# A third set of halves for the expert blocks, a later gelu and a planned transfer rate of 430 for 460 in a PEER decoder block

## The chip, the cores and the metric

The kernel runs on one core of one Trainium2 chip. The metric is device time in microseconds (us), the median of several executions. A profiled execution gives the trace; its span is a little shorter than the time of the same run. Engines are called as in the profile: PE is TensorE's matmul stream and PEld its weight loads, DVE is VectorE, ACT is ScalarE, POOL is GpSimd, SP issues transfers; POOLq, ACTq and SPq are their queues of transfers.

## The reference

One residual layer over 1024 tokens of width 1024, in float32. Three token mixers (stick-breaking attention, dilated window attention, attention into 256 memory tokens) run on a normalised input and are merged by gates. Then comes the expert part, which this change is about:

```python
q = (hf @ w_q).reshape(T, 8, 2, 128)
sc = einsum('thpd,hpkd->thpk', q, subkeys)          # 128 keys a half
s1, i1 = top_k(sc[:, :, 0], 16); s2, i2 = top_k(sc[:, :, 1], 16)
top_s, pos = top_k(all 256 sums s1 + s2, 16)        # 16 experts of 16384 a head
gate = softmax(top_s)
act = gelu(einsum('chkd,cd->chk', u[ic], hc))       # 128 rows of u for every token
out = einsum('chk,chkd->cd', gate * act, v[ic])     # and 128 rows of v
```

So each of the 1024 tokens picks 128 rows (4 KB each) out of the tables u and v, 64 MB each.

## The kernel before

**Two ways through the experts.** The tokens lie in 8 tiles of 128. For six tiles the kernel gathers: a *step* is one chosen expert for each of the 128 tokens, so there are 128 steps a tile and 768 in all. A step fetches a 512 KB block of u rows by an indirect transfer from POOL's queue (`fetch`), multiplies it by the tokens on DVE with a sum (`u<-u,h`, L1129), and 34 steps later (`VLAG`) fetches the v rows; `sum` (L1163) adds four v blocks at a time into two PSUM banks, `poa` and `pob`, on PE with small weights `wz`. Such four are called a group here; there are 192. The gathered rows lie in five u and eight v buffers (`UP`, `VP`), and POOL takes its transfers strictly in the program's order.

For the other two tiles (`DENSE`) the kernel reads both whole tables in 128 blocks of 128 experts: `product` multiplies a block of u with the 256 tokens (24 matmuls, L1184, 128x256), ACT takes the gelu of it (`w<-bank`), `weigh` multiplies it with the gates on DVE, and 12 matmuls 128x512 (L1184 again) add the weighted block of v into four banks. These matmuls are fp32r in three terms, so every operand is split into a high and a low half: ACT copies the high one (`uh`, `vh`, `wh`), DVE subtracts for the low one (`ul`, `vl`, L1264, and `wl`, L1335). The raw blocks `ur` and `vr` come by SP in pairs, 1 MB each, two buffers each; the halves have two buffers each. Blocks 0 to 21 (`RUN`) are multiplied earlier without a split (`early`, fp32 matmuls), so `product(e + 22)` and the v part of block e stand in one round of the loop. In a round ACT has, in this order: `uh` of the next block, the gelu of this one, `wh` and `vh` for the next sum. DVE has `ul`, the gate product `w<-w,g`, `wl` and `vl` for the next sum, and between them the `u<-u,h` of the gather.

**What sets the order.** A planner runs while the program is written. It keeps two clocks, one for PE (`pe`) and one for the transfers (`dma`), and before each step of the gather it puts in dense work until the PE clock has caught up with the other:

```python
least = LEAST * ((len(ex.todo) > 0) + (len(ex.vs) > 0))
due = max(due + least, pe - least)
while filler[0] is not None and (dma > pe or pe < due):
    a, b = fill(1)      # a: PE ns of one piece of dense work, b: its bytes / bw
    pe += a
    dma += b
ex.step()
pe += SUM_NS * (ex.sums - n)
dma += ROW_BYTES * (ex.rows - fetched) / bw[0]
```

`BW = 305.0, 460.0` are the planned rates in bytes a ns: the first until the mixers are done (`front.close()`), the second from there on. ACT and POOL keep the order that the planner writes; PE, DVE and SP are ordered by the framework's scheduler near it. All engines run their own order strictly.

**The gelu of a set.** After every 32 steps a set's 32 activations get their gelu on ACT (`gelu`, `gel<-parts`), are scaled and turned on PE, and become the weights `wz`. In the mixers' time ACT otherwise uses Exp and Ln, so a gelu there stands between two loads of an activation table (L127).

**List buffers.** `sc` (two buffers of 8 KB a partition) holds the key scores of `select`; they are idle once the lists of the last tile are made (`side` is empty).

Of the kernel before, what the change touches and what calls it, by code (L numbers as in the profile page):

```python
# [7 lines left out]
F32 = mybir.dt.float32  # L8
# [9 lines left out]
D = 1024  # L18
# [9 lines left out]
F32R = mybir.dt.float32r  # L28
# [6 lines left out]
RUN = 22  # L35


BW = 305.0, 460.0
SLOW = 1.38, 1.1
SUM_NS, ROW_BYTES = 520.0, 128 * 4096 + 12 * 1024.0  # L40
LEAST = 1500.0
# [38 lines left out]
def block_kernel(ctx: ExitStack, tc: tile.TileContext, io):  # L80
# [4 lines left out]
    sc = pool("sc", 2)  # L85
# [24 lines left out]
    def bank():  # L110
        return ps.tile([128, 512], F32, name="bank")

    def mm(out, lhsT, rhs, **kw):
        n = 1
        for d in rhs.shape[1:]:
            n *= d
        cost[0] += 4 * (n / 2.4 + 2.5) * out.shape[0] / 128
        nc.tensor.matmul(out, lhsT, rhs, **kw)  # L118
# [5 lines left out]
    def actf(out, in_, f, **kw):  # L124
        s = SETS.get(f)
        if s and table[0] != s:
            nc.scalar.preload_act_table_set(s)  # L127
            table[0] = s
        nc.scalar.activation(out, in_, f, **kw)  # L129
# [106 lines left out]
    def load(out, src):  # L236
        count(out)
        nc.sync.dma_start(out, src)
# [836 lines left out]
    class Experts:  # L1075
# [46 lines left out]
        def step(self):  # L1122

            self.run_behind()
            if not self.todo:
                return
            t, k = self.todo.pop(0)
            u = self.us.pop(0)
            nc.vector.scalar_tensor_tensor(u, u, 1.0, t["h"], op0=OP.mult, op1=OP.mult,  # L1129
                                           accum_out=t["parts"][:, k:k + 1])  # L1130
            b, c, j = k // 32, k % 32 // QB, k % QB
            self.behind.append([None] * (VLAG - 1) + [lambda: self.fetch("v", t["iT"][:, c, j, b:b + 1])]
                               + [None] * (SLAG - VLAG - 1) + [(lambda: self.sum(t, b, c, j)) if j % SUMS == SUMS - 1 else None])
            if k % 32 == 31:
                self.behind.append([lambda: self.gelu(t, b), lambda: self.scale(t, b), None,
                                    lambda: self.turn(t), lambda: self.weights(t, 0)])

        def gelu(self, t, b):
# [93 lines left out]
    C = 2  # L1232

    def dense():
        st = ctx.enter_context(ExitStack())
        dp = st.enter_context(tc.tile_pool(name="dp", bufs=2))
        late_pool.append(dp)
        while len(stored) < ND:
            cost[0] += 1500
            yield  # L1240
        wait[0] = True
        whole = dp.tile([128, C, D], F32, name="vr")
        for i in range(ND):
            load(whole[:, i].rearrange("p (k t) -> p k t", k=KD), h2d[i])
        hh = dp.tile([128, KD, TD], F32R, name="hh", bufs=1)
        hl = dp.tile([128, KD, TD], F32R, name="hl", bufs=1)

        def split_tokens():
            for i in range(ND):
                r = whole[:, i].rearrange("p (k t) -> p k t", k=KD)  # L1250
                c = slice(i * 128, (i + 1) * 128)
                actf(hh[:, :, c], r, AF.Copy)
                nc.vector.tensor_sub(hl[:, :, c], r, hh[:, :, c])

        def raw(src, name):
            r = dp.tile([128, C, D], F32, name=name)
            load(r, src)
            return r

        def split(r, x, name):  # L1260
            hi = dp.tile([128, D], F32R, name=name + "h")
            lo = dp.tile([128, D], F32R, name=name + "l")
            actf(hi, r[:, x], AF.Copy)
            nc.vector.tensor_sub(lo, r[:, x], hi)  # L1264
            return hi, lo

        ur, us, ws, vr, gts = {}, {}, {}, {}, {}

        def near(e):
            if e % C == 0:  # L1270
                ur[e // C + 1] = raw(io["uT"][e // C + 1], "ur") if e + C < 128 else None
            return ur[e // C]

        def take(e):
            us[e] = split(near(e), e % C, "u")

        def early(e):
            a = bank()[:, :TD].rearrange("p (i t) -> p i t", i=ND)
            u = near(e)
            for k in range(KD):  # L1280
                mm(a, u[:, e % C, k * 128:(k + 1) * 128], whole[:, :, k * 128:(k + 1) * 128], start=k == 0,
                   stop=k == KD - 1)
            w = ws[e] = dp.tile([128, TD], F32, name="w", bufs=RUN + 2)
            actf(w.rearrange("p (i t) -> p i t", i=ND), a, AF.Gelu)

        def product(e, a):
            if e + 1 < 128:
                take(e + 1)
            uh, ul = us.pop(e)
            for k in range(KD):  # L1290
                kc = slice(k * 128, (k + 1) * 128)
                mmr(a, uh[:, kc], hh[:, k, :], start=k == 0, stop=False, skip_group_check=True)
                mmr(a, ul[:, kc], hh[:, k, :], start=False, stop=False, skip_group_check=True)
                mmr(a, uh[:, kc], hl[:, k, :], start=False, stop=k == KD - 1, skip_group_check=True)
            w = ws[e] = dp.tile([128, TD], F32, name="w", bufs=RUN + 2)
            actf(w, a, AF.Gelu)

        def gate_load(b):
            if b < 16:
                gts[b] = dp.tile([128, TD // 32, 8, 32], F32, name="g")  # L1300
                load(gts[b], gd[:, :, 8 * b:8 * b + 8, :].rearrange("b p i t -> p b i t"))

        ur[0] = raw(io["uT"][0], "ur")
        e = steps = 0
        while next(gates) < ND:
            steps += 1
            cost[0] += 800
            if e < RUN and steps % 5 == 0:
                early(e)
                e += 1  # L1310
            yield
        split_tokens()
        early(e)
        gate_load(0)
        vr[0] = raw(io["vd"][0], "vr")
        for e in range(e + 1, RUN):
            yield
            early(e)
        take(RUN)
        yield  # L1320
        behind[0], wait[0] = True, False

        sums = [[bank() for _ in range(2)] for _ in range(ND)]
        ab = bank().rearrange("p (x n) -> p x n", x=2)

        def weigh(e):
            if e % 8 == 0:
                gate_load(e // 8 + 1)
            w = ws.pop(e)
            nc.vector.tensor_mul(w.rearrange("p (b t) -> p b t", t=32), w.rearrange("p (b t) -> p b t", t=32),  # L1330
                                 gts[e // 8][:, :, e % 8, :])
            wh = dp.tile([128, TD], F32R, name="wh")
            wl = dp.tile([128, TD], F32R, name="wl")
            actf(wh, w, AF.Copy)
            nc.vector.tensor_sub(wl, w, wh)  # L1335
            if e % C == 0:
                vr[e // C + 1] = raw(io["vd"][e // C + 1], "vr") if e + C < 128 else None
            return wh, wl, *split(vr[e // C], e % C, "v")

        now = weigh(0)  # L1340
        for e in range(128):
            if e + RUN < 128:
                product(e + RUN, ab[:, e % 2, :])
                yield
            nxt = weigh(e + 1) if e < 127 else None
            wh, wl, vh, vl = now
            for i in range(ND):
                c = slice(i * 128, (i + 1) * 128)
                for half in range(2):
                    o = sums[i][half]  # L1350
                    f = slice(half * 512, (half + 1) * 512)
                    mmr(o, wh[:, c], vh[:, f], start=e == 0, stop=False, skip_group_check=True)
                    mmr(o, wh[:, c], vl[:, f], start=False, stop=False, skip_group_check=True)
                    mmr(o, wl[:, c], vh[:, f], start=False, stop=e == 127, skip_group_check=True)
                yield
            now = nxt
        for i in range(ND):
            r = dp.tile([128, C, D], F32, name="ur")[:, 0]
            load(r, xres[DENSE[i]])
            for half in range(2):  # L1360
                f = slice(half * 512, (half + 1) * 512)
                nc.vector.tensor_add(r[:, f], r[:, f], sums[i][half])
            nc.sync.dma_start(io["out"][DENSE[i]], r)

    ready, side, stored, late_pool, chosen = [], [], [], [], []
# [11 lines left out]
    def rest():  # L1377
# [15 lines left out]
        front.close()  # L1393
        slow[0], bw[0] = SLOW[1], BW[1]
        yield from dense()

    filler = [rest()]
    slow, bw = [SLOW[0]], [BW[0]]
    pe = dma = due = 0.0
# [14 lines left out]
    while ex.done < NT - ND or filler[0] is not None:  # L1414
        if ex.more():
# [3 lines that stand above are left out]
                a, b = fill(1)  # L1419
                pe += a  # L1420
                dma += b
            n = ex.sums
# [4 lines left out]
        else:  # L1427
            a, b = fill(1)
# [56 lines left out]
```

## Time and profile before

| | |
|---|---|
| time, median of 3 | 3656.19 us (3655.71 to 3662.34) |
| profiled execution: its time, its span | 3664.29 us, 3662.5 us |
| busy in the span: PE, DVE, ACT, POOL | 87%, 63%, 27%, 48% |
| moved | 1182.29 MB, mean 323 GB/s |
| of it by POOL's queue (gathered rows) | 805.40 MB, 221184 packets |
| of it by SP's queue | 336.37 MB |

The profiled execution took 1.8 us more than its span, and 8.1 us more than the median of the runs. Times below are in us from the start of the span. In the views, a stretch's row gives the busy us of each engine with the number of its instructions, the clock that TensorE was granted as a share of full speed, the mean busy share of the 16 DMA engines and the GB/s that they moved. In a row of waits the engine and line that waited stand on the left, and what came last on the right, with the total, the number of times and the longest.

### The profile page before, as it was taken

To read this page: it belongs to the slowest core of one execution; us is meant where nothing else is said; L and a number is where in the kernel's file an instruction comes from. 1 tells how busy PE (TensorE), PEld (TensorE's weight loads), DVE (VectorE), ACT (ScalarE), POOL (GpSimd) and SP (SyncE) were. 2 spreads that over 40 slices of the span, in tenths; PEclk is the share of its full clock that TensorE was granted. 3 is DMA by queue.
4 is the path that set the end of the run, shared out by engine and by line. 5 is a ranking of instruction groups with operands and counts; after the bars stand their busy time and mean duration, and the time that the engine had idled before them with its cause. 6 is when DMAs were issued, how large, how long until landed. Compare 5 with 4: busy or idle time off the path is not lost.

```text
span 3662.5 us, 59007 instructions
## 1 busy us (share of the span) xinstructions
PE 3182.7 (87%) x22418; PEld 2381.9 (65%) x22418; DVE 2295.9 (63%) x5873; ACT 994.8 (27%) x2065; POOL 1764.4 (48%) x1543
## 2 busy tenths in 40 slices
PE   7999979988999889899889898946867888889899
PEld 6889856655556666666555557734655767777677
DVE  5443597555444568886655554889756766666645
ACT  4442223332100123342322111111222333333334
POOL 0000046645565555566454555356656665655540
PEclk9999989998999999999999999968888999999999
DMA  4435678989899997899887999879999999999995
GB/s 160 123 117 169 209 250 327 370 308 342 307 384 366 391 348 278 309 343 374 299 317 279 364 360 377 300 277 393 389 387 398 410 409 402 379 385 392 382 358 180
DMA packets 343084, 1182.29 MB, mean 323 GB/s; under 512 B 38480, under 2 KB 79952, under 8 KB 323344
## 3 DMA queue, kind: packets, MB, share of 16 engines
q0 software_dynamic: 221184, 805.40, 58.2%
q1 hardware_dynamic: 100848, 336.37, 25.2%
q10 hardware_dynamic: 20768, 36.74, 2.6%
q8 instruction: 177, 2.90, 0.3%
q14 instruction: 107, 0.88, 0.1%
HBM read 1140.61 MB, written 37.75 MB: 322 GB/s over the span
## 4 chain that ended last, share of the span: by engine, by line
PE 46%; DMA 17%; DVE 13%; issue 13%; POOL 5%; ACT 2%; another core or an unknown queue 2%; ACTq 0%; SPq 0%; POOLq 0%; DVEq 0%
PE bank L118 31%; PE bank L1184 8%; DMA u<-in_u,iI 7%; DMA v<-in_v,iT 6%; DVE u L1129 3%; POOL v L1085 3%; PE poa L1163 3%; PE pob L1163 3%; POOL u L1085 2%; PE bank L122 1%; DMA ur<-in_uT 1%; DMA w<-in_w_gate 1%; ACT e L129 1%; DVE ab L1208 1%
## 5 line engine op out<-in xcount | busy, mean ns | idle before, releaser
L1085 POOL DMA_INDIRECT u<-in_u,iI x768 | 881.0, 1147 | 950.8 <-DVE wide L330 471.9
L1129 DVE SCALAR_TENSOR_TENSOR u<-u,h 128x1024 f32<-128x1024 f32 x768 | 933.3, 1220 | 605.8 <-DMA u<-in_u,iI 508.9
L1085 POOL DMA_INDIRECT v<-in_v,iT x768 | 882.7, 1149 | 853.1 <-PE pob L1163 349.5
L118 PE MATMUL bank<-wide,w 128*128 128x384 f32 x1536 | 523.3, 495 | 14.2 <-DVE wide L330 5.3
L118 PEld LDWEIGHTS bank<-wide,w 128*128 128x128 f32 x1536 | 292.3, 193 | 219.1 <-issue 21.3
L118 PE MATMUL bank<-w,wide 128*128 128x128 f32 x2304 | 277.2, 279 | 20.4 <-issue 17.5
L118 PEld LDWEIGHTS bank<-w,wide 128*128 128x128 f32 x2304 | 267.7, 194 | 35.4 <-issue 28.0
L1163 PE MATMUL pob<-v,wz 128*32 128x256 f32 x3072 | 231.8, 414 | 66.7 <-DMA v<-in_v,iT 61.0
L1184 PE MATMUL bank<-hh,uh 128*128 128x256 f32 x848 | 244.3, 288 | 30.4 <-ACT uh L129 19.0
L1184 PE MATMUL bank<-vl,wh 128*128 128x512 f32 x512 | 212.5, 415 | 51.4 <-DVE vl L1264 42.1
L118 PE MATMUL bank<-big,w 128*128 128x256 f32 (+1 forms) x1280 | 244.1, 347 | 10.7 <-issue 9.1
L1184 PE MATMUL bank<-hh,ul 128*128 128x256 f32 x848 | 243.0, 287 | 11.6 <-DVE ul L1264 10.6
L1163 PE MATMUL poa<-v,wz 128*32 128x256 f32 x3072 | 217.8, 405 | 29.1 <-DMA v<-in_v,iT 20.9
L1184 PE MATMUL bank<-hl,uh 128*128 128x256 f32 x848 | 242.0, 285 | 0.0
L118 PEld LDWEIGHTS bank<-big,w 128*128 128x128 f32 x1280 | 210.0, 196 | 43.7 <-issue 21.6
L129 ACT ACTIVATE e<-bank 128x512 f32<-128x512 f32 (+2 forms) x208 | 110.0, 529 | 448.2 <-PE bank L118 296.2
L1184 PE MATMUL bank<-vh,wh 128*128 128x512 f32 x512 | 212.2, 415 | 0.7 <-ACT vh L129 0.7
L1184 PE MATMUL bank<-vh,wl 128*128 128x512 f32 x512 | 208.3, 407 | 0.0
L1163 PEld LDWEIGHTS pob<-v,wz 128*32 128x32 f32 x3072 | 101.1, 117 | 162.3 <-issue 61.8
L129 ACT ACTIVATE w<-bank 128x256 f32<-128x256 f32 x128 | 49.1, 385 | 573.9 <-PE bank L1184 412.1
L1184 PEld LDWEIGHTS bank<-hh,uh 128*128 128x128 f32 x848 | 164.8, 194 | 40.5 <-ACT uh L129 19.1
L1163 PEld LDWEIGHTS poa<-v,wz 128*32 128x32 f32 x3072 | 98.4, 115 | 124.4 <-issue 47.6
(292 smaller groups left out, 5508.8 us busy)
## 6 DMA issues: line engine op xcount, KB each, us to landing
ur<-in_uT SPq DMA_DIRECT2D x64, 1024.0 KB
vr<-in_vd SPq DMA_DIRECT2D x64, 1024.0 KB
w<-in_w_in SPq DMA_DIRECT2D x102, 512.0 KB
w<-in_w_gate SPq DMA_DIRECT2D x72, 512.0 KB
w<-in_w_pq SPq DMA_DIRECT2D x48, 512.0 KB
g<-gd SPq DMA_DIRECT2D x16, 1024.0 KB
w<-in_w_o SPq DMA_DIRECT2D x48, 256.0 KB
w<-in_w_out SPq DMA_DIRECT2D x24, 512.0 KB
```

The source lines that it names most:

```text
L118: nc.tensor.matmul(out, lhsT, rhs, **kw)
L122: nc.tensor.transpose(out, in_, ident)
L129: nc.scalar.activation(out, in_, f, **kw)
L1085: nc.gpsimd.indirect_dma_start(out=t, out_offset=None, in_=io[kind], in_offset=bass.IndirectOffsetOnAxis(ap=ap, axis=0))
L1129: nc.vector.scalar_tensor_tensor(u, u, 1.0, t["h"], op0=OP.mult, op1=OP.mult, accum_out=t["parts"][:, k:k + 1])
L1163: nc.tensor.matmul(o[32 * k:32 * k + 32], t["wz", c][:, x, :], vs[y][:, 256 * k:256 * k + 256], start=b == 0 and x == SUMS - 1 and c % 2 == 0,
L1184: nc.tensor.matmul(out, lhsT, rhs, **kw)
L1208: nc.vector.tensor_scalar(ab[:, 0, x], iota, sl[:, 0, t + x:t + x + 1], sl[:, 2, t + x:t + x + 1], op0=OP.is_equal, op1=OP.mult)
```

## The change

It has three parts.

1. The halves of a u block are made two blocks ahead and not one: `product(e)` calls `take(e + 2)`, and `take(RUN + 1)` is added at the start. The halves of v likewise, in a new `take_v`, which `weigh(e)` calls for block e + 1. Blocks whose number leaves 2 when divided by 3 put both halves into one `sc` buffer, once `side` is empty; until then, and for the other blocks, the two buffers of before are used.
2. The planned rate `BW[1]` is 430 and not 460.
3. The gelu of a set, and what follows from it, come two steps later.

```diff
-BW = 305.0, 460.0
+BW = 305.0, 430.0
...
             if k % 32 == 31:
-                self.behind.append([lambda: self.gelu(t, b), lambda: self.scale(t, b), None,
+                self.behind.append([None, None, lambda: self.gelu(t, b), lambda: self.scale(t, b), None,
                                     lambda: self.turn(t), lambda: self.weights(t, 0)])
...
-        def split(r, x, name):
-            hi = dp.tile([128, D], F32R, name=name + "h")
-            lo = dp.tile([128, D], F32R, name=name + "l")
+        def split(r, x, name, n):
+            if n % 3 == 2 and not side:
+                both = sc.tile([128, 16, 128], F32, name="sc").rearrange("p a b -> p (a b)").bitcast(F32R)
+                hi, lo = both[:, :D], both[:, D:]
+            else:
+                hi = dp.tile([128, D], F32R, name=name + "h")
+                lo = dp.tile([128, D], F32R, name=name + "l")
             actf(hi, r[:, x], AF.Copy)
             nc.vector.tensor_sub(lo, r[:, x], hi)
             return hi, lo
...
         def product(e, a):
-            if e + 1 < 128:
-                take(e + 1)
+            if e + 2 < 128:
+                take(e + 2)
...
         take(RUN)
+        take(RUN + 1)
...
+        vs = {}
+
+        def take_v(e):
+            if e % C == 0:
+                vr[e // C + 1] = raw(io["vd"][e // C + 1], "vr") if e + C < 128 else None
+            vs[e] = split(vr[e // C], e % C, "v", e)
...
             actf(wh, w, AF.Copy)
             nc.vector.tensor_sub(wl, w, wh)
-            if e % C == 0:
-                vr[e // C + 1] = raw(io["vd"][e // C + 1], "vr") if e + C < 128 else None
-            return wh, wl, *split(vr[e // C], e % C, "v")
-
+            if e + 1 < 128:
+                take_v(e + 1)
+            return wh, wl, *vs.pop(e)
+
+        take_v(0)
         now = weigh(0)
```

POOL's order is the same in both programs. Over the whole program DVE does the 768 `u<-u,h` in both, and its first `vl` stands behind 582 of them in both. From there the orders part. On DVE, in the middle of the dense part, two rounds read so before (`u,parts<-u,h` is the gather's product, the others belong to the dense blocks; the numbers tell buffers apart):

```order
L1264 TENSOR_TENSOR ul_25620<-ur_25422,uh_25619 128x1024
L1129 SCALAR_TENSOR_TENSOR u_25670,parts_21863<-u_25670,h_21861 128x1024
L1330 TENSOR_TENSOR w_25647<-w_25647,g_26461 128x256
L1335 TENSOR_TENSOR wl_25679<-w_24181,wh_25678 128x256
L1264 TENSOR_TENSOR vl_25683<-vr_25459,vh_25682 128x1024
L1264 TENSOR_TENSOR ul_25706<-ur_25559,uh_25705 128x1024
L1129 SCALAR_TENSOR_TENSOR u_25675,parts_21863<-u_25675,h_21861 128x1024
L1129 SCALAR_TENSOR_TENSOR u_25695,parts_21863<-u_25695,h_21861 128x1024
L1330 TENSOR_TENSOR w_25733<-w_25733,g_26461 128x256
L1335 TENSOR_TENSOR wl_25742<-w_24241,wh_25741 128x256
L1129 SCALAR_TENSOR_TENSOR u_25738,parts_21863<-u_25738,h_21861 128x1024
L1264 TENSOR_TENSOR vl_25748<-vr_25601,vh_25747 128x1024
```

and so after, on DVE at the same place:

```order
L1268 TENSOR_TENSOR ul_25109<-ur_24916,uh_25108 128x1024
L1129 SCALAR_TENSOR_TENSOR u_25190,parts_22402<-u_25190,h_22400 128x1024
L1342 TENSOR_TENSOR w_25136<-w_25136,g_25572 128x256
L1347 TENSOR_TENSOR wl_25150<-w_23708,wh_25149 128x256
L1268 TENSOR_TENSOR vl_25154<-vr_24958,vh_25153 128x1024
L1268 TENSOR_TENSOR sc_25199<-ur_25054,sc_25199 128x1024
L1129 SCALAR_TENSOR_TENSOR u_25195,parts_22402<-u_25195,h_22400 128x1024
L1342 TENSOR_TENSOR w_25226<-w_25226,g_26110 128x256
L1347 TENSOR_TENSOR wl_25230<-w_23765,wh_25229 128x256
L1129 SCALAR_TENSOR_TENSOR u_25284,parts_22402<-u_25284,h_22400 128x1024
L1268 TENSOR_TENSOR vl_25236<-vr_25091,vh_25235 128x1024
```

The same two rounds hold four gather products before and three after, and the second `ul` goes into an `sc` buffer (31 blocks of u and 38 of v do). The halves `ul` and `vl` stand at the same places among the others, but are those of the block after the next.

At the end of DVE's order the rows before are these (`ur<-ur,bank` adds the dense sums to the residual):

```order
L1335 TENSOR_TENSOR wl_28271<-w_27804,wh_28270 128x256
L1264 TENSOR_TENSOR vl_28275<-vr_28209,vh_28274 128x1024
L1362 TENSOR_TENSOR ur_28302<-ur_28302,bank_19977 128x512
L1362 TENSOR_TENSOR ur_28302<-ur_28302,bank_19978 128x512
L1362 TENSOR_TENSOR ur_28307<-ur_28307,bank_19979 128x512
L1362 TENSOR_TENSOR ur_28307<-ur_28307,bank_19980 128x512
L1480 UNCONDITIONAL_BRANCH
```

and after, on DVE at the end (`row<-row` adds a quarter of the gather's last tile, `wz<-wT` makes the weights of its next two groups):

```order
L1176 TENSOR_TENSOR row_27963<-row_27963,poa_24330 128x256
L1153 TENSOR_TENSOR wz_28118<-wT_27904,spread_84 128x256
L1347 TENSOR_TENSOR wl_28034<-w_27320,wh_28033 128x256
L1375 TENSOR_TENSOR ur_28090<-ur_28090,bank_19903 128x512
L1375 TENSOR_TENSOR ur_28090<-ur_28090,bank_19904 128x512
L1375 TENSOR_TENSOR ur_28095<-ur_28095,bank_19905 128x512
L1375 TENSOR_TENSOR ur_28095<-ur_28095,bank_19906 128x512
L1176 TENSOR_TENSOR row_28073<-row_28073,poa_24330 128x256
L1153 TENSOR_TENSOR wz_28178<-wT_27904,spread_84 128x256
L1176 TENSOR_TENSOR row_28149<-row_28149,pob_24331 128x256
L1176 TENSOR_TENSOR row_28209<-row_28209,pob_24331 128x256
L1493 UNCONDITIONAL_BRANCH
```

What came last was the dense part and is now the gather. Counted on PE: between the first dense sum and that of block 100 there are 54 groups of gathered rows before and 40 after; before, the last group stands ahead of 25 dense sums, and after, five groups stand behind the last dense sum.

On ACT, in the mixers' time, the later gelu shows so (one piece of the difference):

```order
 L129 ACTIVATE e<-bank 128x512
-L127 ACT_TABLE_LOAD
-L129 ACTIVATE gel<-parts 128x32
-L129 ACTIVATE e<-bank 128x256
-L127 ACT_TABLE_LOAD
+L129 ACTIVATE e<-bank 128x256
 L129 ACTIVATE e<-e 128x256 x2
 L129 ACTIVATE e<-bank 128x512
 L129 ACTIVATE sq<-bank 128x384
 L129 ACTIVATE e<-bank 128x256
+L127 ACT_TABLE_LOAD
+L129 ACTIVATE gel<-parts 128x32
```

The gelu moved behind four more activations; in all ACT has 33 loads of a table before and 29 after.

More of the change, by code (lines that the diff above doesn't have):

```diff
@@ L1274, in take @@
         def take(e):
-            us[e] = split(near(e), e % C, "u")
+            us[e] = split(near(e), e % C, "u", e)
         def early(e):
```

## The prediction

> **What bounds the kernel now.** I read the page's chain first, then the stretches of the second half, then who waits there, then the end of the chain. The page gives one mixture:
>
> ```profile
> PE 46%; DMA 17%; DVE 13%; issue 13%; POOL 5%; ACT 2%; another core or an unknown queue 2%; ACTq 0%; SPq 0%; POOLq 0%; DVEq 0%
> ```
>
> That is an average over stages, so the stretches decide. From 2700 us on they are the dense blocks beside the gather:
>
> ```profile
> core 0: us, PE busy (x) PEld busy (x) DVE busy (x) ACT busy (x) POOL busy (x), PEclk, DMA share, GB/s
> ...
> 2700.00:2800.00 100.00, 74.04 (x552) 58.32 (x552) 65.36 (x111) 25.68 (x39) 57.51 (x44) 0.85 1.03 401
> 2800.00:2900.00 100.00, 79.80 (x616) 64.01 (x616) 68.96 (x109) 34.02 (x53) 68.32 (x54) 0.86 1.01 399
> 2900.00:3000.00 100.00, 84.30 (x606) 68.81 (x603) 64.25 (x100) 31.19 (x49) 60.48 (x49) 0.93 1.02 411
> 3000.00:3100.00 100.00, 87.76 (x644) 71.84 (x645) 68.72 (x107) 32.20 (x50) 57.16 (x47) 0.94 1.03 402
> 3100.00:3200.00 100.00, 84.77 (x591) 68.70 (x589) 64.15 (x99) 31.09 (x48) 55.05 (x44) 0.92 0.99 385
> 3200.00:3300.00 100.00, 88.97 (x648) 71.90 (x648) 63.15 (x99) 31.12 (x49) 55.19 (x48) 0.95 0.99 384
> 3300.00:3400.00 100.00, 87.27 (x642) 71.48 (x641) 66.39 (x101) 31.11 (x49) 56.27 (x43) 0.95 0.98 382
> 3400.00:3500.00 100.00, 86.42 (x610) 68.68 (x609) 61.12 (x92) 31.00 (x48) 51.59 (x44) 0.91 0.97 377
> 3500.00:3600.00 100.00, 96.90 (x813) 78.56 (x806) 42.71 (x62) 33.63 (x53) 37.87 (x36) 1.00 0.85 322
> 3600.00:3662.00 62.00, 57.99 (x256) 47.69 (x254) 36.24 (x45) 27.38 (x40) 0.00 (x0) 1.00 0.48 170
> ```
>
> Read the last two columns downward. For 800 us the DMA engines are full (share 0.97 to 1.03, mean 392.6 GB/s); then 322, then 170. In the last 160 us the load has turned round: TensorE is full (97 of 100 us) and the transfers idle. The end of the chain says the same, in time order:
>
> ```profile
> 3561.12 12.94 DMA v<-in_v,iT
> 3574.20 1.93 PE pob L1163 x32
> 3576.13 5.84 PE bank L1184 x36
> 3581.97 1.86 PE pob L1163 x32
> 3583.83 72.13 PE bank L1184 x339
> 3655.99 2.73 DVE ur L1362 x4
> ```
>
> The gather is over at 3584, and 72 us of dense matmuls follow alone. So the stage is short of transfers first and of TensorE afterwards; it loses by the order of the two.
>
> While the transfers are full, TensorE still waits:
>
> ```profile
> PE bank L1184 <- DVE vl L1264: 42.1, 16, 5.4
> PE pob L1163 <- DMA v<-in_v,iT: 22.0, 5, 7.8
> PE bank L1184 <- ACT uh L129: 19.0, 1, 19.0
> PE poa L1163 <- DMA v<-in_v,iT: 14.5, 4, 8.1
> ...
> PE bank L1184 <- DVE ul L1264: 10.6, 3, 6.1
> PE bank L1184 <- ACT w L129: 9.0, 4, 4.0
> ...
> DVE u L1129 <- DMA u<-in_u,iI: 207.8, 74, 8.5
> ...
> POOL v L1085 <- PE pob L1163: 124.2, 25, 13.4
> POOL v L1085 <- PE poa L1163: 65.0, 22, 8.4
> ```
>
> (2715 to 3583 us.) DVE waits 208 us for gathered u rows with `vl` and `ul` queued behind, and that is why TensorE finds no halves; POOL waits 189 us for TensorE to free v buffers.
>
> **The change part by part.**
>
> *The rate 430 for 460.* It removes no instruction; it moves dense work ahead of the gather. By the order of PE, the first 100 dense sums have 40 groups of gathered rows among them and not 54, and five groups come behind the last dense sum where 25 sums stood behind the last group. DVE's 582 gather products ahead of the first `vl` are the same in both, so I take the time up to 2700 us as unmoved by it, and the bytes behind that point as equal: (401+399+411+402+385+384+382+377+322) x 0.1 + 170 x 0.062 = 356.8 MB in 962.5 us, 371 GB/s on average. If the engines now stay full nearly to the end, the stage takes 356.8 MB divided by the full rate, and a tail. Rate: bounds are 377 (the poorest of the eight full stretches) and 403 (mean of the first four); I take 390, which is 382 at share 0.98 brought to a share of 1.00, since the last four stretches are the steady state. That gives 915 us.
>
> The tail: behind the last dense sum 20 v rows are left, 8 of them in flight, 10.5 MB or 27 us at 390, which the 915 us hold already. On top come the last group's matmuls (1.86), the additions and the stores, one after another, since there is one `row` buffer: add, store, load the next quarter, add, store. What such a turn costs shows in SP's waits:
>
> ```profile
> SPq L1174 <- DMA out<-row: 64.4, 7, 14.3
> ```
>
> 9.2 us each under full transfers. Bounds: 6.5 us, which is what stood behind the last matmul before (3656.0 to 3662.5), and 45 us, if all five waits of the three last quarters (three stores, two loads) cost 9 us behind the last row. I take 18: two turns, for most overlap with the 27 us.
>
> Sum: 915 + 18 = 933 us against 962.5, a gain of 29.
>
> *Can TensorE keep up?* A block costs 5.84 us by the row with 36 matmuls (24 of a product, 12 of a sum), a group 1.86. For 100 blocks and 40 groups that is 584 + 74 = 658 us. Their transfers, by
>
> ```profile
> ur<-in_uT SPq DMA_DIRECT2D x64, 1024.0 KB
> vr<-in_vd SPq DMA_DIRECT2D x64, 1024.0 KB
> ...
> g<-gd SPq DMA_DIRECT2D x16, 1024.0 KB
> ```
>
> are 112.5 pieces of 1.05 MB and 320 gathered blocks of 0.52 MB, 286 MB or 733 us at 390. So TensorE needs 90% of it, where before it was 584 + 100 of some 867 us. The waits of before, without the 19 us at the start of the stage, are 98 us in 868, or 83 in 733; 658 + 83 = 741 would make TensorE the bound by a hair.
>
> *The third set.* It takes nothing away on ACT and DVE (as many copies and subtractions), adds no transfer, and makes the raw buffers of `ur` and `vr` free one block earlier, so SP asks a block earlier too. What it buys is one more block (5.84 us) between asking and use, more than any of the 16 waits for `vl` (longest 5.4) and all but the longest for `ul`. I take those 52.7 us as gone from TensorE, 45 in 733; bounds: none gone, or all with the clock beside it. (Both kinds of half cost 1.2 us on DVE.)
>
> ```profile
> L1129 DVE SCALAR_TENSOR_TENSOR u<-u,h 128x1024 f32<-128x1024 f32 x186 | 226.7, 1221 | 226.4 <-DMA u<-in_u,iI 207.8 <-issue 14.8 <-DMA h<-h2s 3.3
> ...
> L1264 DVE TENSOR_TENSOR vl<-vr,vh 128x1024 fp32r<-128x1024 f32 x104 | 126.9, 1221 | 7.8 <-ACT vh L129 6.0 <-issue 1.7
> ```
>
> What is late next is `wl`: it is still made for the very next sum and stands behind the same u rows, one `vl` (1.2 us) earlier than what TensorE awaited before. So waits shorter than about 2 us vanish and longer ones shrink; with 658 + 38 to 60 us TensorE stays under 733. The set's own gain is therefore not added to the 29; it is what lets the 29 happen. An `sc` buffer, a third buffer and a second one are all free when asked for: each was last used by the product or sum just before, as in the two-buffer scheme.
>
> The clock helps. After a wait the matmuls run slower for a while:
>
> ```profile
> 3000.32 0.63 PE L1184 MATMUL bank<-vh,wl 128*128 128x512 f32 x1
> ...
> 3000.74 0.63 PE L1184 MATMUL bank<-vh,wh 128*128 128x512 f32 x1
> ...
> 3008.90 0.40 PE L1184 MATMUL bank<-vl,wh 128*128 128x512 f32 x1
> ...
> 3009.14 0.39 PE L1184 MATMUL bank<-vh,wl 128*128 128x512 f32 x1
> ```
>
> 0.42 us from start to start just after a wait of 2.8 us, 0.24 us eight us later, and the granted clock is 0.91 to 0.95 in the waiting stretches and 1.00 in the full one. By the Trainium skill ("TensorE: Matmul & The Clock Gate", Part 1) the array falls to half rate after an idle window of about 3.4 us and returns after a busy one; the trace agrees in the factor (0.42 to 0.24), not in the length, since 2.8 us sufficed. By that rule the 733 us could regain up to 8% of TensorE's time, and the rival below in which TensorE starves the transfers would be worth less; the sum stays.
>
> *The gelu two steps later.* It issues nothing new. In the dense stage ACT waited for a set once for long:
>
> ```profile
> ACT gel L129 <- issue: 21.8, 1, 21.8
> ```
>
> and over the whole span it loads tables so (count, busy us, ns of one):
>
> ```profile
> L127 ACT ACT_TABLE_LOAD x32 | 41.1, 1283 | 0.6
> ```
>
> Two steps are about 9 us here (186 steps in some 800 us), so up to 9 us of that one wait; TensorE's answer to it was one wait of 6 us for `ul`. In the mixers' time ACT gets four table loads fewer (1.28 us each, 5 us on an engine 27% busy) and the neighbouring work shifts; the weights still come ahead of their first sum. I cost it at 0, cover being the full transfers, with -6 to +6 for the reshuffled front.
>
> **The rivals.** (a) *Slower: TensorE starves the gather.* Now 2.5 dense blocks stand between groups, so v buffers come free later, POOL waits longer and holds back the u rows behind, and the engines run dry. For it speak POOL's 189 us and the fall from 411 to 377 as TensorE's share rose; against it that TensorE needs 90% only. It decides where the mean rate falls under 356.8/(962.5-18) = 378; at 370 the stage takes 982, 20 slower.
>
> (b) *The wait only moves from `vl` to `wl`*, so the rate stays at the last four stretches' 382: 934 + 18 = 952, a gain of 10.
>
> (c) *The tail takes the 45 us*: 915 + 45 = 960, no change.
>
> (d) *The set does more*: at the first four stretches' 403, 885 + 18 = 903, a gain of 59.
>
> (e) *A ceiling on the core's reads* that holds the stage at its old mean of 371: 962 + 18 = 980, 18 slower, whatever the order. Eight rows of 377 to 411 speak against it, and I give it 1 in 100. The Trainium skill ("DMA: Bandwidth & Descriptors", Specifications) names such a ceiling, about 358 GB/s from HBM for one core; by it the estimate would be 997 + 18, a loss of 52, but the trace exceeds it for 800 us.
>
> **How the numbers follow.** The forecast (gains of 12 to 48) gets 0.50, (a) 0.14, (b) 0.14, (c) 0.08, (d) 0.13, (e) 0.01. The span of the profiled run falls from 3662.5 to about 3633. Its own time was 3664.29, 8.1 above the median 3656.19; the gain is carried over to the median: 3656 - 29 = 3627. The range reaches from (d), 3598, to 3662, a little past no change, and leaves out (a) beyond 6 us and (e). What a measurement can tell here is about 0.2%, 7 us: faster are the forecast, (d) and three quarters of (b), 0.74; the same the rest of (b) and (c), 0.12; slower 0.14.
>
> **What would show it.** Right: the stretches from 2700 us stay at 385 GB/s or more until about 40 us before the end; TensorE is near 95% there; its waits for `vl` and `ul` fall under 15 us; dense sums end ahead of the gather. Wrong: a share under 0.96 in the steady stretches with longer waits of POOL for `poa` and `pob` (a), new waits for `wl` (b), a long idle end with `row` (c), or a stage that starts at another time than 2700.

## The result and the profile after

| | before | after |
|---|---|---|
| time, median of 20 runs each, same chip | 3660.42 us | 3640.43 us |
| ratio, 95% interval | | 0.9942 (0.9921 to 0.9964) |
| profiled execution: its time, its span | 3664.29, 3662.5 us | 3641.01, 3639.2 us |

The forecast was 3627 us, a gain of 29. Measured are 0.58% (0.36 to 0.79), some 21 us; the profiled spans differ by 23.3. Direction and size hold here; a second measurement of the same kernel, told of below, gives less. What the experiments changed is the account of where the gain comes from.

The stretches of the kernel after, with the columns as before:

```profile
core 0: us, PE busy (x) PEld busy (x) DVE busy (x) ACT busy (x) POOL busy (x), PEclk, DMA share, GB/s
2700.00:2800.00 100.00, 75.83 (x546) 62.68 (x547) 68.00 (x113) 30.34 (x45) 51.94 (x41) 0.85 1.03 402
2800.00:2900.00 100.00, 89.24 (x637) 72.80 (x637) 68.48 (x105) 36.44 (x57) 53.49 (x43) 0.95 0.99 389
2900.00:3000.00 100.00, 92.02 (x681) 75.59 (x680) 68.54 (x104) 35.98 (x55) 52.10 (x43) 0.98 1.02 401
3000.00:3100.00 100.00, 90.81 (x659) 76.19 (x658) 64.05 (x100) 33.93 (x53) 54.40 (x46) 0.97 0.98 375
3100.00:3200.00 100.00, 86.85 (x608) 73.12 (x607) 63.72 (x96) 33.65 (x53) 45.81 (x41) 0.91 0.97 375
3200.00:3300.00 100.00, 96.02 (x724) 79.88 (x722) 69.05 (x104) 34.41 (x55) 57.81 (x48) 1.00 1.00 394
3300.00:3400.00 100.00, 89.57 (x639) 74.51 (x639) 69.47 (x106) 36.45 (x57) 52.19 (x41) 0.95 0.97 380
3400.00:3500.00 100.00, 92.72 (x697) 76.40 (x696) 65.67 (x101) 34.91 (x55) 58.36 (x47) 0.98 0.98 387
3500.00:3600.00 100.00, 91.29 (x595) 66.03 (x597) 58.05 (x90) 31.75 (x48) 49.79 (x46) 0.97 0.94 360
3600.00:3639.00 39.00, 17.53 (x188) 7.71 (x180) 3.00 (x7) 0.00 (x0) 14.98 (x16) 0.76 0.78 285
```

The two last rows are what the change is seen by: 360 and 285 GB/s where 322 and 170 stood, and no end in which TensorE is busy alone. The eight rows above them show its price: their mean is 387.9 GB/s, below the 392.6 of before. TensorE is busier in them, 89 of 100 us on average against 84.

Who waits from 2700 to 3600 us, after:

```profile
PE bank L1184 <- DVE wl L1347: 52.6, 27, 6.2
PE bank L1184 <- DVE ul L1268: 19.6, 1, 19.6
...
PE bank L1184 <- DVE vl L1268: 6.2, 4, 3.4
...
POOL v L1085 <- PE pob L1163: 165.6, 25, 20.8
POOL v L1085 <- PE poa L1163: 117.2, 24, 16.1
...
DVE u L1129 <- DMA u<-in_u,iI: 214.0, 94, 7.6
```

TensorE's waits for `vl` are down from 42.1 us to 6.2, and 52.6 us for `wl` have come in their place. (The one of 19.6 for `ul` opens the stage, as 19.0 for `uh` did.) POOL waits 283 us for TensorE to free v buffers, where it was 189.

The end, in order of time, on PE (the figure in brackets is the idle time before):

```profile
3602.35 0.39 PE L1184 MATMUL bank<-vh,wl 128*128 128x512 f32 x1
...
3613.01 3.64 PE L1163 MATMUL pob<-v,wz 128*32 128x256 f32 x32 [7.98 <-DMA v<-in_v,iT]
3618.75 1.93 PE L1163 MATMUL pob<-v,wz 128*32 128x256 f32 x32 [2.10 <-DMA v<-in_v,iT]
3624.91 3.64 PE L1163 MATMUL pob<-v,wz 128*32 128x256 f32 x32 [4.23 <-DMA v<-in_v,iT]
3630.20 3.64 PE L1163 MATMUL pob<-v,wz 128*32 128x256 f32 x32 [1.65 <-DMA v<-in_v,iT]
```

The last dense sum is done at 3602.7, and 36.5 us of gathered v rows, additions and stores follow. The chain of waits ends so (start, us):

```profile
3632.75 1.87 DMA row<-xres
...
3634.80 0.42 DVE row L1176
```

**A measure for the experiments.** All parts of the change but the gelu act in the dense stage. Its start is the first `ul<-ur` on DVE, so its length is the span less that time. In these answers for the tile `ur` the two times behind the durations are the first and last start; in order, the kernels before, after, after again (below) and with the gelu alone (below):

```profile
L1264 DVE TENSOR_TENSOR ul<-ur,uh x106: 1167/1218/1226, 2716.2 to 3588.8; 128x1024 fp32r<-128x1024 f32 x106
```

```profile
L1268 DVE TENSOR_TENSOR ul<-ur,uh x75: 1212/1220/1229, 2715.3 to 3498.2; 128x1024 fp32r<-128x1024 f32 x75
```

```profile
L1268 DVE TENSOR_TENSOR ul<-ur,uh x75: 1212/1220/1228, 2740.7 to 3523.9; 128x1024 fp32r<-128x1024 f32 x75
```

```profile
L1264 DVE TENSOR_TENSOR ul<-ur,uh x106: 1211/1219/1242, 2744.0 to 3617.6; 128x1024 fp32r<-128x1024 f32 x106
```

The stage starts anywhere from 2705 to 2744 us over the fourteen profiles, but its length repeats: 946.3 us before (3662.5 - 2716.2) and 947.5 with the gelu alone; 923.9 after and 926.1 after again. So in the two pairs that can be compared, single profiles of a stage differ by 1 to 2 us, where times of the whole kernel scatter by 20 and more.

| kernel | ratio to before (95%) | stage, us | mean GB/s, 2700 to 3500 |
|---|---|---|---|
| before | 1 | 946.3 | 392.6 |
| after | 0.9942 (0.9921 to 0.9964) | 923.9 | 387.9 |
| after_again | 0.9991 (0.9965 to 1.0018) | 926.1 | 386.6 |
| e1_rate_only | 1.0073 (1.0046 to 1.0101) | 986.3 | 368.4 |
| e2_set_only (460) | 0.9941 (0.9917 to 0.9964) | 928.4 | 401.3 |
| e3_gelu_only | 1.0008 (0.9983 to 1.0032) | 947.5 | 393.4 |
| e4_no_gelu (set, 430) | 0.9917 (0.9886 to 0.9949) | 923.8 | 386.6 |
| e8_rate_445 | 0.9934 (0.9908 to 0.9960) | 920.8 | 395.4 |
| e11_v_only (460) | 0.9948 (0.9922 to 0.9974) | 927.1 | 400.6 |
| e5_fewer_bytes | 0.9832 (0.9794 to 0.9871) | 885.5 | 369.4 |
| e6_less_pe | 0.9889 (0.9852 to 0.9926) | 891.3 | 400.8 |
| e7_w_ahead | 0.9896 (0.9859 to 0.9933) | 905.5 | 396.4 |
| e10_rows | 0.9886 (0.9854 to 0.9919) | 897.5 | 399.5 |
| e13_rows_445 | 0.9843 (0.9806 to 0.9880) | 894.5 | 404.4 |

Each ratio is to the kernel before on the same chip in the same session, over all runs; it is not just the quotient of the medians (for after_again that would be 3669.64 / 3680.13 = 0.997). One execution of e13 that took 5434 us at a granted clock of 0.69 is left out of its ratio. Four sessions were run: the first for the result, then e1, e2, e4 and e7; then e5, e6, e8 and e10; then after_again, e3, e11 and e13.

### The profile page after: what moved, and what is told of

Read it like the earlier page. It is cut to its first block, busy times and chain, and to the rows that moved or that the text cites. A ratio compares the mean times of both kernels' runs of the same rounds, so it can differ in the third digit from the quotient of the medians.

```text
span 3639.2 us, 58882 instructions
## 1 busy us (share of the span) xinstructions
PE 3173.4 (87%) x22418; PEld 2376.4 (65%) x22418; DVE 2292.6 (63%) x5873; ACT 992.1 (27%) x2061; POOL 1760.4 (48%) x1543
## 4 chain that ended last, share of the span: by engine, by line
PE 40%; DMA 18%; issue 17%; DVE 13%; POOL 7%; ACT 2%; another core or an unknown queue 2%; ACTq 0%; SPq 0%; POOLq 0%; DVEq 0%
PE bank L118 28%; DMA u<-in_u,iI 8%; PE bank L1184 6%; DMA v<-in_v,iT 6%; POOL u L1085 4%; DVE u L1129 4%; POOL v L1085 3%; PE pob L1163 3%; PE poa L1163 2%; DMA g<-gd 1%; PE bank L122 1%; DMA gd<-g 1%; DVE ab L1208 1%; ACT e L129 1%
## 5 line engine op out<-in xcount | busy, mean ns | idle before, releaser
L1085 POOL DMA_INDIRECT u<-in_u,iI x768 | 869.5, 1132 | 949.6 <-DVE wide L330 471.6
L118 PE MATMUL bank<-big,w 128*128 128x256 f32 (+1 forms) x1280 | 236.2, 339 | 8.6 <-issue 8.3
L1163 PE MATMUL poa<-v,wz 128*32 128x256 f32 x3072 | 206.7, 396 | 11.9 <-DMA v<-in_v,iT 8.1
L1184 PE MATMUL bank<-hh,ul 128*128 128x256 f32 x600 | 172.2, 287 | 19.6 <-DVE ul L1268 19.6
L1184 PE MATMUL bank<-vh,wl 128*128 128x512 f32 x360 | 149.4, 415 | 40.3 <-DVE wl L1347 40.2
L1184 PE MATMUL bank<-hh,uh 128*128 128x256 f32 x600 | 172.8, 288 | 10.0 <-ACT w L129 8.5
L1184 PE MATMUL bank<-hl,uh 128*128 128x256 f32 x600 | 172.1, 287 | 0.0
L1184 PE MATMUL bank<-vh,wh 128*128 128x512 f32 x360 | 150.4, 418 | 3.7 <-ACT wh L129 3.6
L1184 PE MATMUL bank<-vl,wh 128*128 128x512 f32 x360 | 146.8, 408 | 7.4 <-DVE vl L1268 6.2
L118 PE MATMUL bank<-oT,w 128*128 128x384 f32 (+1 forms) x480 | 152.0, 455 | 0.0
```

Source lines behind the costliest of these rows:

```text
L1085: nc.gpsimd.indirect_dma_start(out=t, out_offset=None, in_=io[kind], in_offset=bass.IndirectOffsetOnAxis(ap=ap, axis=0))
L1163: nc.tensor.matmul(o[32 * k:32 * k + 32], t["wz", c][:, x, :], vs[y][:, 256 * k:256 * k + 256], start=b == 0 and x == SUMS - 1 and c % 2 == 0,
```

## The experiments

In the expectations A is the prediction's account: the gain is the order that 430 gives, and the set only lets it happen. B is that the halves made earlier are the gain; C that the later gelu is; D that with the set in place the rate matters little.

**The rate alone** (e1_rate_only), the kernel before with one number changed:

```diff
-BW = 305.0, 460.0
+BW = 305.0, 430.0
```

> The kernel before with the planned rate 430 and nothing else of the change. Theory A (the gain is one of order: dense work moves from the end, where the transfers idle, to where they are full, and the transfers are the bound): most of the change's gain of 0.58% (21 us), 10 to 25 us faster, with the stretches from 2700 to 3500 us at 380 GB/s or more and 5 groups or so behind the last dense sum. Theory B (the halves come too late; only with the third set can TensorE take the denser order): within 8 us of before, with TensorE's waits for vl well over 42 us and the stretches under 380 GB/s.

It came out 0.7% slower, and its stage 40 us longer. Its stretches, from 2800, and its waits:

```profile
2800.00:2900.00 100.00, 85.75 (x602) 69.83 (x601) 60.51 (x95) 31.23 (x49) 47.64 (x43) 0.91 0.98 377
2900.00:3000.00 100.00, 87.78 (x600) 71.20 (x600) 62.72 (x94) 31.00 (x48) 42.51 (x37) 0.91 0.93 352
3000.00:3100.00 100.00, 87.44 (x614) 71.76 (x613) 61.86 (x96) 33.70 (x53) 49.40 (x43) 0.95 0.93 359
...
3500.00:3600.00 100.00, 87.90 (x566) 68.02 (x565) 61.38 (x96) 29.66 (x46) 45.35 (x40) 0.91 0.86 319
3600.00:3700.00 100.00, 80.00 (x593) 52.54 (x592) 35.19 (x53) 20.85 (x31) 41.06 (x41) 0.85 0.85 319
```

```profile
PE bank L1184 <- DVE vl L1264: 96.0, 35, 5.0
...
POOL v L1085 <- PE pob L1163: 178.0, 21, 17.8
POOL v L1085 <- PE poa L1163: 161.9, 21, 17.1
```

This is the prediction's rival (a), in the kernel without the set: TensorE waits 96 us for `vl` and not 42, frees v buffers late, POOL stands 340 us and not 189, and the DMA engines, full before, have a share of 0.93 to 0.98 from 2800 to 3500 us. Inside the traces the rate falls behind POOL's waits. With 2750 to 3500 us cut into pieces of 5 us, the piece next after one that POOL spent for more than half in waiting for TensorE moves 323 GB/s on average here, and all others 393; it is 357 and 400 before, 350 and 405 after. The order by itself is a loss.

**The set alone** (e2_set_only): the kernel after with the rate of 460 and the gelu at its old place.

```diff
-BW = 305.0, 430.0
+BW = 305.0, 460.0
...
-                self.behind.append([None, None, lambda: self.gelu(t, b), lambda: self.scale(t, b), None,
+                self.behind.append([lambda: self.gelu(t, b), lambda: self.scale(t, b), None,
```

> The change with the rate back at 460 and the gelu where it was: only the third set, two blocks ahead. Theory A: within 8 us of before, since the 72 us of dense sums alone at the end stay, though TensorE's waits for vl shrink from 42 us to under 10 and waits for wl of about 40 us come up. Theory B: 10 to 25 us faster.

```profile
3200.00:3300.00 100.00, 87.52 (x679) 71.27 (x681) 70.04 (x110) 34.02 (x53) 67.11 (x50) 1.00 1.02 409
3300.00:3400.00 100.00, 87.60 (x645) 71.90 (x638) 64.30 (x100) 33.29 (x53) 58.47 (x48) 0.97 1.01 399
3400.00:3500.00 100.00, 89.77 (x669) 72.70 (x668) 69.10 (x108) 31.25 (x49) 59.14 (x46) 0.98 1.03 409
3500.00:3600.00 100.00, 97.76 (x817) 77.25 (x816) 44.73 (x64) 34.61 (x55) 37.68 (x36) 0.98 0.88 339
```

```profile
PE bank L1184 <- DVE wl L1347: 50.8, 26, 6.5
...
POOL v L1085 <- PE poa L1163: 75.6, 22, 19.0
POOL v L1085 <- PE pob L1163: 68.4, 22, 9.6
...
3582.11 72.78 PE bank L1184 x339
```

The set alone gives 0.9941, as much as the whole change as far as the ratios tell (its stage is 4.5 us longer), though the end of 72.78 us in which TensorE works alone is still there. What it bought is a mean of 401 GB/s for 393, most of it in the rows from 3200 to 3500: 399 to 409, where the kernel before had 377 to 384. (The row before them, 372, is below the 385 of before.) POOL's waits fall from 189 us to 144. A's claim that the set adds nothing of its own falls; B and D stand.

How the set raises the rate is not shown in full. TensorE's waits for halves, without the one that opens the stage, do not shrink at 460: they are 53 us before and 52 here, now nearly all for `wl`. (At 430 they fall, from 102 in e1 to 62 in the kernel after.) And in pieces of 5 us as above, those behind POOL's waits move 359 GB/s and the others 407, where before these had 400: a part of the gain lies where POOL was not held. The set also makes raw `ur` and `vr` buffers free a block earlier, so that SP can ask earlier; no run separates that from the halves' being early.

**The set with 430 and the gelu at its old place** (e4_no_gelu), against the kernel after:

```diff
-                self.behind.append([None, None, lambda: self.gelu(t, b), lambda: self.scale(t, b), None,
+                self.behind.append([lambda: self.gelu(t, b), lambda: self.scale(t, b), None,
```

> The change with the gelu of a set where it was before: third set and rate 430. Both theories A and B: the same as the changed kernel within 6 us, a ratio to before of 0.992 to 0.997. A third theory C (the later gelu frees ACT, whose wait of 21.8 us for a set went away): 8 us or more slower than the changed kernel, a ratio of 0.997 or above.

Its stage is that of after to 0.1 us (923.8), and the gelu alone, put into the kernel before, does nothing that these runs can tell:

```diff
-                self.behind.append([lambda: self.gelu(t, b), lambda: self.scale(t, b), None,
+                self.behind.append([None, None, lambda: self.gelu(t, b), lambda: self.scale(t, b), None,
```

> The kernel before with the gelu of a set two steps later and nothing else. All theories but one: within 6 us of before. Theory C (ACT's wait for a set holds the dense halves up): 8 us or more faster.

1.0008 (0.9983 to 1.0032), stage 947.5 against 946.3. C falls. The interval leaves room for 6 us of gain to 12 of loss.

**A rate between** (e8_rate_445), the kernel after with 445:

```diff
-BW = 305.0, 430.0
+BW = 305.0, 445.0
```

> The changed kernel with a planned rate of 445, between the two. With the third set the order only trades a lone end of TensorE's (72 us at 460) against slower stretches (388 GB/s at 430, 401 at 460). If the rate is near its best anywhere between (theory D: with the set the rate matters little): ratio to before 0.990 to 0.996, within 10 us of the changed kernel, about half the dense sums left alone at the end. If the denser order itself is worth the gain (theory A): halfway, 3 to 10 us slower than the changed kernel but faster than the set at 460.

0.9934, stage 920.8. With the set, 460, 445 and 430 give stages of 928, 921 and 924 to 926 us, and ratios whose intervals overlap; 12 of the 25 dense sums are left alone at the end at 445. A denser order shortens the lone end and loses as much in the stretches (401, 395, 387 GB/s), and more dense work between groups holds v buffers longer: POOL's waits for TensorE are 144 us at 460, 222 at 445 and 283 at 430. Whether the few us between the rates are real is not settled.

**The third set for v alone** (e11_v_only): the kernel before with `take_v`, and `u` as before.

```diff
-            us[e] = split(near(e), e % C, "u")
+            us[e] = split(near(e), e % C, "u", 0)
...
+        def take_v(e):
...
+            vs[e] = split(vr[e // C], e % C, "v", e)
```

> The kernel before (rate 460, gelu as it was) with the third set and the second block ahead for v alone; the halves of u stay one block ahead in two buffers. If the halves of v are what came late (42 us of the waits before, against 11 for those of u): the gain of the whole set, ratio 0.992 to 0.997, waits for vl under 10 us. If both are needed, because TensorE then waits for ul: 0.997 or more, waits for ul of 20 us or more.

0.9948, stage 927.1 against 928.4 with both; POOL's waits are 161 us. The set of u gives nothing that these runs can tell. TensorE waits for `ul` 28.2 us in 15 times instead of for `wl` (5.9 us in 6), with the same length of stage.

**Less to move and less to multiply.** In e5_fewer_bytes every second pair of v blocks isn't loaded (33.6 MB less; its output uses the pair before), in e6_less_pe a third of the dense sums' matmuls, `wh` by `vl`, is left out.

```diff
-                vr[e // C + 1] = raw(io["vd"][e // C + 1], "vr") if e + C < 128 else None
+                nxt = e // C + 1
+                if nxt % 2 and e + C < 128:
+                    vr[nxt] = vr[e // C]
+                    count(vr[nxt])
+                else:
+                    vr[nxt] = raw(io["vd"][nxt], "vr") if e + C < 128 else None
```

> The changed kernel, but every second pair of v blocks isn't loaded: its halves are made from the pair before, so those sums are of other data. 32 transfers of 1.05 MB go, 33.6 MB of the 357 MB behind 2700 us, 87 us at 388 GB/s; every matmul, copy and subtraction stays, and the planner still counts the bytes, so the order stays. If the transfers set the pace of the changed kernel's dense part (theory A): 50 to 87 us faster than the changed kernel, ratio to before 0.970 to 0.980. If TensorE or the halves do (theory B): under 25 us faster, ratio 0.987 or more, and the stretches' GB/s fall by a tenth.

```diff
-                    mmr(o, wh[:, c], vl[:, f], start=False, stop=False, skip_group_check=True)
+                    cost[0] += 512 / 2.4 + 3
```

> The changed kernel without the matmuls of the weights' high half with v's low half: 512 matmuls of 0.23 us fewer, 117 us of TensorE's work, the output that much less exact; the planner still counts them, all else stays. Theory A (transfers): under 25 us faster than the changed kernel, ratio 0.987 or more. Theory B (TensorE's own work): 50 us or more faster, ratio under 0.980.

33.6 MB are 87 us at 388 GB/s, and the stage fell by 38 (923.9 to 885.5). The matmuls left out are 117 us of TensorE, and it fell by 33 (19 by the ratios, which is within theory A's 25; e5's ratio lies between its two theories). Without them the wait that TensorE has grows:

```profile
PE bank L1184 <- DVE wl L1347: 97.9, 44, 9.3
```

and without the bytes the DMA engines are no longer full in some stretches:

```profile
3000.00:3100.00 100.00, 90.32 (x639) 75.23 (x638) 62.79 (x97) 34.09 (x54) 46.89 (x43) 0.93 0.89 333
3100.00:3200.00 100.00, 86.43 (x620) 72.31 (x619) 63.83 (x97) 31.67 (x50) 47.88 (x40) 0.91 0.92 350
```

So neither is the one bound of the stage after the change; each saved microsecond of either buys less than half of one.

**The next late operand** (e7_w_ahead): `wh` and `wl` also a block further ahead, in three buffers.

```diff
-            wh = dp.tile([128, TD], F32R, name="wh")
-            wl = dp.tile([128, TD], F32R, name="wl")
+            wh = dp.tile([128, TD], F32R, name="wh", bufs=3)
+            wl = dp.tile([128, TD], F32R, name="wl", bufs=3)
...
-            nxt = weigh(e + 1) if e < 127 else None
-            wh, wl, vh, vl = now
+            if e + 2 < 128:
+                weigh(e + 2)
+            wh, wl, vh, vl = *hs.pop(e), *vs.pop(e)
```

> The change, with wh and wl of a sum made two blocks ahead as well (three buffers each), so that TensorE's new waits for wl (52.6 us in the trace) go. Theory A: the waits fall under 10 us, the time moves by less than 8 us against the changed kernel (ratio to before 0.990 to 0.996), since the transfers set the pace. Theory B (the halves bound): 15 to 50 us faster than the changed kernel, ratio under 0.990.

The waits for `wl` are gone and the stage is 18 us shorter than after (905.5). The raw blocks are asked for in the same rounds of the loop as after, so here only the operand is earlier. The ratio, 0.9896, stands at the border of the two theories and is not told apart from the 0.9917 of e4 on the same chip; the gain is seen in the stage. What TensorE waits for next is the gelu of ACT, 40.8 us:

```profile
PE bank L1184 <- ACT w L129: 40.8, 10, 7.0
```

POOL's waits fall from 283 to 217 us.

**Rows** (e10_rows): e7 with three `row` buffers, loaded a quarter ahead, and stores that are issued three steps later. The space comes from two buffers of `w`.

```diff
-                t["row"] = gw.tile([128, 256], F32, name="row", bufs=1)
-                for k, src in enumerate(quarters(xres[t["n"]], c)):
-                    nc.sync.dma_start(t["row"][32 * k:32 * k + 32], src)
+                for x in ([0, 1], [2], [3], [])[c]:
+                    t["row", x] = gw.tile([128, 256], F32, name="row", bufs=3)
+                    for k, src in enumerate(quarters(xres[t["n"]], x)):
+                        nc.sync.dma_start(t["row", x][32 * k:32 * k + 32], src)
...
+                self.behind.append([None] * 3 + [lambda: self.store(t, c)])
```

> The changed kernel with three more steps: wh and wl made two blocks ahead (as in the run on that), three row buffers for one, so that a quarter's residual is loaded a quarter ahead, and the stores of a quarter issued three steps after its addition. In the changed kernel SP waited 31 us for stores of rows with table loads behind, ACT stood behind stores that waited for an addition, and the end had a chain of store, load, add. Theory A (transfers run dry where their queues are held up): stretches at 395 GB/s or more, no wait of SP for out<-row, 10 to 25 us faster than the changed kernel, ratio 0.983 to 0.992. Theory B (pace set by TensorE): within 6 us of the run with wh and wl ahead.

897.5, 8 us less than e7; SP has no wait for a store of `row` left up to 3600 us, where it had 31 us after. The ratio, 0.9886, is not told apart from e7's 0.9896, and of the 26 us that this stage is under after, 18 came with e7 already.

**The same with 445** (e13_rows_445), one number changed from e10:

```diff
-BW = 305.0, 430.0
+BW = 305.0, 445.0
```

> The run with wh and wl ahead and three row buffers, at a rate of 445 for 430. If transfers are near their floor there (357 MB at 400 GB/s are 893 us of the 910 that the run with 430 took behind 2700 us), the rate has nothing left to give: ratio to before 0.984 to 0.992, 5 to 25 us faster than the changed kernel of this call. If the dense order still costs transfers: under 0.984.

```profile
3200.00:3300.00 100.00, 91.08 (x683) 75.59 (x682) 68.92 (x105) 36.63 (x55) 59.95 (x47) 0.98 1.02 411
3300.00:3400.00 100.00, 91.83 (x684) 75.89 (x683) 67.08 (x101) 36.37 (x57) 60.51 (x48) 0.98 1.03 409
3400.00:3500.00 100.00, 92.00 (x703) 76.40 (x701) 72.29 (x113) 36.73 (x56) 60.11 (x48) 1.00 1.01 402
```

The lowest ratio of the kernels that compute everything: 0.9843 (0.9806 to 0.9880), stage 894.5 (52 us under before). It lies at the border of the two expectations, and neither the ratio nor the 3 us of stage tell it apart from e10. From 3200 to 3500 us it holds 402 to 411 GB/s with TensorE busy for 91 to 92 of 100 us; the lowest of the eight stretches is 390.

**The kernel after once more** (after_again), unchanged, in the last session:

> The changed kernel itself, on one chip with the three runs beside it, to compare them without going by way of other chips: ratio to before 0.992 to 0.997.

0.9991 (0.9965 to 1.0018): here the whole kernel's gain could not be told from none. Its profile says where: the stage is 926.1 us long, 21 shorter than that of e3 on the same chip, which has no third set (947.5), but it began at 2740.7 and not 2715.3. The start varies without the later gelu too: 2708.3 to 2733.0 in e4, e1 and e2 on one chip. On the chip of after_again, the three kernels with the later gelu began at 2727.9 to 2744.0 and e11, which has it at its old place, at 2716.6. The later gelu acts ahead of the stage and may cost time there: from the 351st to the 401st product `u<-u,h` DVE takes 202 to 206 us in the five profiles with the gelu at its old place, and 208 to 223 in the nine with the later one. Part of that is made up again; the starts average 2718.8 and 2725.0 and scatter by more than this difference. So a small cost of the third part is neither shown nor excluded, and why the gain in the stage did not reach the times of that session stays open. The gain of the stage is shown in both profiles of the kernel; of the whole time the two sessions together leave anything from 0.2% slower to 0.8% faster.

## Why the prediction was right, and where it was not

- **The bound and the bytes.** Right. Behind 2700 us 357.4 MB were moved (forecast 356.8), and the time up to there was unmoved: the stage began at 2715.3 and 2716.2 in the first two profiles.
- **The sum of 933 us.** Measured 939 from 2700 on. The rate was sized at 390 GB/s up to the end; 346.3 MB up to 3600 took 900 us and not 888, since the stretches gave 388 and the last of them 360: 12 us lost. The tail was sized at 27 of rows and 18 of turns, 45 behind the last dense sum, and took 36.5: some 8 us won back (that the two misses have opposite signs is luck): the chain's end shows one load of `row` and the last add behind the rows, and not two turns of some 9 us each.
- **"The set's own gain is therefore not added to the 29; it is what lets the 29 happen."** This step failed. Half of it holds: without the set the order loses 40 us (e1). But the set alone gives 18 us of stage (e2), nearly all of the 22, and v's alone as much. So that the total came near was in part luck: at 460 the same time is had without the order that the 29 were worked out from. I priced the 52.7 us of waits as TensorE's, of whose time a saved microsecond buys a third at most (e6). What the set raised is the rate of the transfers, 393 to 401 GB/s at 460 and 368 to 388 at 430. A part of that goes by way of v buffers and POOL's queue, as its waits beside the rate show: 340, 283 and 217 us at 368, 388 and 396 GB/s in e1, after and e7, which have the same planned rate. How much goes that way, and how much by raw blocks that are asked for earlier, stays open. A price at the transfers stood in the rows shown, as the fall from 411 to 377 GB/s over the stage beside POOL's 189 us.
- **TensorE keeps up at 90%.** Nearly: 91 of 100 us from 2800 to 3500, not the 95 forecast, with a granted clock of 0.91 to 1.00. Two of the eight stretches gave 375 and one 380 GB/s, under the 385 that was to show the forecast right.
- **`wl` is late next.** Right in kind, wrong in size: I took waits shorter than 2 us as vanishing, and 52.6 us came back, as many as the 52.7 taken as gone. The prediction names new waits for `wl` as the sign of rival (b); they came, but without (b)'s rate. One `vl` less ahead of it saves 1.2 us, and the wait of DVE for u rows that delays both is up to 7.6.
- **The gelu at 0.** Right as far as e3 and e4 tell; a small cost ahead of the stage is not excluded (see after_again).
- **The rivals.** (a) is true without the set and partly with it: POOL's waits grew to 283 us and the mean of the eight stretches fell by 5 GB/s to 387.9, which is above its 378. (b) describes the waits, but the rate was above its 382. (c) was too dear. (d)'s rate of 403 came, at 460 (401), where the lone end of TensorE took back what it gave. The ceiling of (e), which the Trainium skill ("DMA: Bandwidth & Descriptors", Specifications) puts at about 358 GB/s for one core, as half of a stack's 716, is not seen here, where one core runs: e13 held a mean of 404 for 800 us.

## What to carry to other kernels

Where engines with strict queues feed one another in a ring, an operand that arrives late can cost more than the wait shows, since what the waiting engine holds goes on to hold the next queue; look for the price at the resource that is full, here in the GB/s of a stretch. Give each part of a change its own price even if another part needs it: two parts of which one loses 40 us and one wins 18 won 22 together. And where the start of a stage wanders from run to run, compare the stage's length in the traces beside the times, and ask of every part that acts ahead of the stage whether it moves the start.

## What the runs showed of the hardware

- The transfers of one core ran at up to 411 GB/s, at a share of 1.02 of its DMA engines. The share does not give the rate by itself: in the kernel after, 0.98 stood beside 375 and beside 387 GB/s.
- Short waits late in the program were dear for TensorE: of the last groups, the one after 2.10 us of idling took 1.93 us, those after 4.23 and 7.98 took 3.64, and so did one after 1.65 us that followed such a slow group. The granted clock in that stretch was 0.76. The Trainium skill ("TensorE: Matmul & The Clock Gate", Part 1) has half rate after an idle window of about 3.4 us; the trace agrees for the groups after 2.10, 4.23 and 7.98 us, while 2.8 us sufficed in the stage of before.
